# 96 unused bytes at the top of on-chip memory, which shift one half of the tiles against the other

## The chip, the cores and the metric

The kernel runs on one core of a Trainium2 chip. The metric is the device time of one launch in microseconds (us). Before the change the median of three runs is 1282.69 us (1281.51 to 1283.05). The engines are named as in the profile: PE is TensorE (matmul), PEld its loading of weights, DVE VectorE, ACT ScalarE, POOL GpSimd, SP SyncE, which issues most DMAs.

## The reference

One sequence of 256 tokens with 1024 features passes two transformer blocks, all in float32:

```
x = x + (sigmoid(ga) * (att @ w_att_o) + sigmoid(gr) * (ret @ w_ret_o)) @ w_out   # att, ret from rms_norm(x) @ w_in
x = x + (silu(h @ w_gate) * (h @ w_up)) @ w_down                                  # h = rms_norm(x), 2816 hidden
x = rms_norm(x)
x = x + concat(gated_mlp, banded_attention) @ w_out2                              # from rms_norm(x) @ w_in2
q = h @ w_query; top 16 of 128 x 128 sub-keys per head, 8 heads, softmax g         # h = rms_norm(x)
x = x + sum over the chosen experts of g * gelu(u_e . h) * v_e                     # 16384 experts
```

The last line is computed densely: every token meets all 16384 rows of `u` (the first layer), a gate that is zero for experts not chosen multiplies the result, and all 16384 rows of `v` follow (the second layer). Those two layers are 128 units of 128 experts each.

## The kernel before

**Three products for one.** A float32 matrix is split into two parts, `hi` (the value as the reduced float32 type that PE takes at full rate) and `lo` (the rest). A product of two such matrices is hi*hi + hi*lo + lo*hi. Weights come from memory in units of 128 x 1024 numbers: SP loads a unit into a `raw` tile (4 buffers), ACT copies it to `whi` (L95), DVE subtracts to get `wlo` (L96). Activations are split in the same way into pairs of tiles: `act`, `hid`, `att`, `xbh` and `xbl` in the stages up to the experts' first layer, `keys` and `q` in the second layer.

**Four shapes of matmul.** In each, one operand is loaded into PE beforehand (the stationary one, 128 x 128) and the other streams past it (the moving one, 128 x 256 or 128 x 512). The four shapes are called by letters from here on:

- **D**, `mm3` from `gemm_t` and `gemm_k` (L110 to L112): stationary `whi` or `wlo`, moving 256 columns of an activation. 24 of them per unit. It is the experts' first layer, the query product and a part of the other stages.
- **C**, `mm2` from `gemm_w` (L118, L119): stationary `whi`, moving 512 columns (hi and lo of an activation beside each other), then stationary `wlo`, moving 256 columns. Gates, gate/up/down of the feed-forward.
- **B**, `mm3` from `gemm_n` (L110 to L112 again, but with 512 columns): stationary an activation, moving 512 columns of `whi` or `wlo`.
- **A**, `second_layer` in `peer` (L1121): stationary `keys` or `q` (the gated activations), moving 512 columns of `whi` or `wlo`.

**Where tiles lie.** A partition of the on-chip memory is filled from both ends. Pools opened as usual lie at the low end, and pools opened under `using_default_side("right")` at the high end, each new one below the last. `run` opens the pool of weights `wb` first at the high end, and with it the `raw` tiles. Later high-end pools are `wa` (more weights), and in `peer` `gs`, `query` (with `keys` and `q`), `hold`, `topk`, `gelu`, `comb`, `gates` and the last `x3`. Activations (`act`, `hid`, `att`, `xbh`, `xbl`), residuals and the work tiles of blocks 1 and 2 are at the low end. All tiles that PE reads in the shapes A to D begin at a multiple of 256 bytes of their own half's start, so within a half their addresses agree modulo 256. In the program as it is built they are 0 modulo 256 for the low end and 224 modulo 256 for the high end (`whi` at byte 163808, for one). So the addresses of the shapes are, modulo 256:

| shape | moving | stationary | stationary minus moving |
|---|---|---|---|
| A | 224 | 224 | 0 |
| B | 224 | 0 | 32 |
| C, D | 0 | 224 | 224 (32 behind) |

**Order.** The order of work on each engine is set by a scheduler at build time from priorities; weights run ahead (`high_priority(offset=AHEAD)` in `unit`). The choice of experts on DVE is cut into steps, and `pump` lets a number of them out after each first-layer unit.

Of the kernel before, what the change touches and what calls it, by code (L numbers as in the profile page):

```python
# [7 lines left out]
F32 = mybir.dt.float32  # L8
# [35 lines left out]
class Net:  # L44
# [195 lines left out]
    def run(self):  # L240
        self.wpools, self.turn = [], 0
        with self.tc.using_default_side("right"):
            self.weights("wb", self.stack, 4, 3)
        self.xbp = self.pool("xb", 1)
        with ExitStack() as st:
            actp = self.pool("actp", 2, st)
            self.res = self.pool("res", 2, st)
            self.work = self.pool("work", 2, st)
            with ExitStack() as sw:
                with self.tc.using_default_side("right"):  # L250
                    self.weights("wa", sw, 0, 3)
                x2, h, acc, acg = self.block1(actp)
                x3, h, acc = self.block2(actp, x2, h, acc, acg)
            self.wpools.pop()
            self.peer(st, x3, h, acc)
# [985 lines left out]
```

## Time and profile before

| | |
|---|---|
| median of three runs | 1282.69 us |
| the profiled execution | 1281.63 us |
| its span | 1279.8 us |
| PE busy | 1269.9 us, 8408 matmuls |
| PEld busy | 1152.2 us, 8408 loads |
| DVE, ACT, POOL busy | 927.6, 740.0, 268.6 us |

The span runs from the first to the last record of the trace. A matmul's busy time is modelled and reaches past the start of the next, so the duration of one (279 to 391 ns) says little about its rate; the rate is read from the distance between the starts of matmuls that follow each other without a wait. In the views below a row of a window gives the number of matmuls that touch it. With a window of W and a duration d of one, that number times the distance between starts is W + d.

### The profile page before, as it was taken

The page shows a single profiled execution, that of the slowest core. Times are in us where ns is not written, and L with a number is a line of the kernel's source. Part 1 is how long each engine was busy: PE and PEld are TensorE (multiplying, and loading weights), DVE is VectorE, ACT ScalarE, POOL GpSimd, SP SyncE. Part 2 cuts the span into 40 slices and gives each one's busy share as a digit, 9 for nine tenths or more (in the row PEclk, how much of TensorE's full clock was granted, in tenths as well). Part 3 has the DMA queues.
Part 4 walks back from the last instruction along what each step waited for, and adds up shares of the span by engine and source line. Part 5 has one row for each costly group of instructions (what it writes and reads, how often), then busy time and mean ns, then how long its engine had stood idle before and what let it go on. Part 6 is the DMA issues. An engine that isn't in the chain of part 4 may idle for free.

```text
span 1279.8 us, 22295 instructions
## 1 busy us (share of the span) xinstructions
PE 1269.9 (99%) x8408; PEld 1152.2 (90%) x8408; DVE 927.6 (72%) x1857; ACT 740.0 (58%) x1238; POOL 268.6 (21%) x173
## 2 busy tenths in 40 slices
PE   8999999999999999999999999999999999999998
PEld 8978889888988889999999999999988888888887
DVE  7867787777777876987995566676566666666665
ACT  5555565655555776545554676666455555555553
POOL 2000000000000000018877778772000000000000
PEclk9999999999999999999999999999999999999999
DMA  7735558966667535567767677776666766666664
GB/s 242 268 132 165 181 182 324 315 193 189 180 186 225 162 111 164 173 193 191 184 158 209 182 169 179 165 169 179 217 216 214 219 220 219 215 219 219 221 198 157
DMA packets 91068, 252.94 MB, mean 198 GB/s; under 512 B 26960, under 2 KB 29008, under 8 KB 90832
## 3 DMA queue, kind: packets, MB, share of 16 engines
q1 hardware_dynamic: 68960, 241.58, 59.7%
q0 software_dynamic: 20992, 8.46, 6.0%
q8 instruction: 66, 1.08, 0.3%
q10 hardware_dynamic: 1008, 1.47, 0.3%
q14 instruction: 42, 0.34, 0.1%
HBM read 240.93 MB, written 10.55 MB: 196 GB/s over the span
## 4 chain that ended last, share of the span: by engine, by line
PE 94%; DVE 4%; DMA 1%; ACT 1%; issue 0%; DVEq 0%; ACTq 0%
PE ax L1121 27%; PE mm L110 15%; PE mm L112 14%; PE mm L111 14%; PE mm L118 13%; PE mm L119 7%; DVE wlo L96 1%; PE ax L994 1%; ACT whi L95 0%; PE ax L940 0%; DVE itop L793 0%; DMA x3t<-xt 0%; DMA small<-in_small_dram 0%; PE ax L484 0%; PE ax L730 0%
## 5 line engine op out<-in xcount | busy, mean ns | idle before, releaser
L96 DVE TENSOR_TENSOR wlo<-raw,whi 128x1024 fp32r<-128x1024 f32 (+2 forms) x433 | 524.2, 1213 | 235.3 <-ACT whi L95 233.5
L95 ACT ACTIVATE whi<-raw 128x1024 fp32r<-128x1024 f32 (+3 forms) x439 | 457.6, 1046 | 299.9 <-PE mm L111 133.9
L110 PE MATMUL mm<-xbh,whi 128*128 128x256 f32 x1104 | 311.9, 283 | 0.0
L112 PE MATMUL mm<-xbh,wlo 128*128 128x256 f32 x1104 | 308.3, 279 | 0.4 <-DVE wlo L96 0.3
L111 PE MATMUL mm<-xbl,whi 128*128 128x256 f32 x1104 | 308.3, 279 | 0.2 <-DVE xbl L177 0.2
L884 POOL DMA_INDIRECT cmat<-best,pos x128 | 240.6, 1880 | 221.2 <-DVE itop L793 161.6
L112 PEld LDWEIGHTS mm<-xbh,wlo 128*128 128x128 f32 x1104 | 207.4, 188 | 1.2 <-DVE wlo L96 1.0
L111 PEld LDWEIGHTS mm<-xbl,whi 128*128 128x128 f32 x1104 | 207.5, 188 | 0.4 <-DVE xbl L177 0.4
L110 PEld LDWEIGHTS mm<-xbh,whi 128*128 128x128 f32 x1104 | 207.6, 188 | 0.2 <-ACT xbh L176 0.2
L118 PE MATMUL mm<-act,whi 128*128 128x512 f32 x512 | 178.5, 391 | 0.0
L1121 PE MATMUL ax<-whi,q 128*128 128x512 f32 x513 | 158.2, 389 | 0.0
L1121 PE MATMUL ax<-wlo,keys 128*128 128x512 f32 x513 | 158.1, 389 | 0.0
L1121 PE MATMUL ax<-whi,keys 128*128 128x512 f32 x513 | 158.1, 389 | 0.0
L119 PE MATMUL mm<-act,wlo 128*128 128x256 f32 x512 | 144.4, 282 | 0.0
L176 ACT ACTIVATE keys<-S 128x256 fp32r<-128x256 f32 x128 | 53.4, 418 | 151.4 <-PE ax L1121 151.4
L118 PEld LDWEIGHTS mm<-act,whi 128*128 128x128 f32 x512 | 96.1, 188 | 20.4 <-DVE gu L132 0.3
L1121 PEld LDWEIGHTS ax<-whi,q 128*128 128x128 f32 x513 | 96.3, 188 | 20.0
L1121 PEld LDWEIGHTS ax<-wlo,keys 128*128 128x128 f32 x513 | 96.3, 188 | 19.9
L1121 PEld LDWEIGHTS ax<-whi,keys 128*128 128x128 f32 x513 | 96.2, 188 | 19.9
L119 PEld LDWEIGHTS mm<-act,wlo 128*128 128x128 f32 x512 | 96.8, 189 | 0.0
L111 PE MATMUL mm<-act,whi 128*128 128x256 f32 x328 | 91.9, 281 | 2.3 <-DVE act L275 2.3
L110 PE MATMUL mm<-act,whi 128*128 128x256 f32 x328 | 92.9, 284 | 0.8 <-DVE qkv L314 0.6
(291 smaller groups left out, 1667.5 us busy)
## 6 DMA issues: line engine op xcount, KB each, us to landing
raw<-in_peer_u_dram SPq DMA_DIRECT2D x128, 512.0 KB, 3.7
raw<-in_peer_v_dram SPq DMA_DIRECT2D x128, 512.0 KB, 4.2
raw<-in_w_in_b_dram SPq DMA_DIRECT2D x32, 512.0 KB, 4.5
raw<-in_w_in_a_dram SPq DMA_DIRECT2D x31, 512.0 KB, 3.6
raw<-in_w_gate_dram SPq DMA_DIRECT2D x22, 512.0 KB, 5.5
raw<-in_w_up_dram SPq DMA_DIRECT2D x22, 512.0 KB, 4.2
raw<-in_w_out_dram SPq DMA_DIRECT2D x16, 512.0 KB, 4.3
cmat<-zero SPq DMA_DIRECT2D x16, 512.0 KB, 6.8
```

Of the source, the lines that this page charges most:

```text
L95: self.last_copy = nc.scalar.activation(hi[:, s], raw[:, s], AF.Copy).ins
L96: low = (engine or nc.vector).tensor_tensor(out=lo[:, s], in0=raw[:, s], in1=hi[:, s].bitcast(F32), op=OP.subtract)
L110: mm(ps, lhsT=left[0], rhs=right[0], start=first, stop=False)
L111: mm(ps, lhsT=left[0], rhs=right[1], start=False, stop=False)
L112: mm(ps, lhsT=left[1], rhs=right[0], start=False, stop=last)
L118: mm(ps, lhsT=weight[0], rhs=both, start=first, stop=False)
L119: mm(ps[:, :T], lhsT=weight[1], rhs=both[:, 0], start=False, stop=last)
L176: nc.scalar.activation(hi, src, AF.Copy)
L884: i = nc.gpsimd.indirect_dma_start(self.cmat, bass.IndirectOffsetOnAxis(ap=ps[:, hd, 1, k:k + 1], axis=0), bs[:, hd, 1, k:k + 1], None, co ...
L994: nc.tensor.matmul(C[:, t * 128:t * 128 + 128], lhsT=A[:, t], rhs=G[i][:, t], start=i == 0, stop=i == 1)
L1121: nc.tensor.matmul(banks[tb][o // 512][:, o % 512:o % 512 + e - o], lhsT=s[left][:, ts], rhs=w[right][:, o:e], start=first, stop=end and e ...
```

## The change

Before the first high-end pool is opened, one more is opened there, with one tile of 24 float32 numbers (96 bytes) in each partition. Nothing writes or reads it. It stays open to the end.

```diff
         with self.tc.using_default_side("right"):
+            self.pool("edge", 1).tile([128, 24], F32, name="edge")
             self.weights("wb", self.stack, 4, 3)
```

All tiles of the high end move down by 96 bytes and nothing else moves: `whi` from byte 163808 to 163712, `keys` from 182240 to 182144, `raw` from 212960 to 212864. High-end tiles are now 128 modulo 256. The instructions on every engine, their order and their waits are those of the kernel before, one for one. The table becomes:

| shape | moving | stationary | stationary minus moving |
|---|---|---|---|
| A | 128 | 128 | 0 |
| B | 128 | 0 | 128 |
| C, D | 0 | 128 | 128 |

## Rows read from the trace of the kernel before

**Rows 1.** The page's head and busy time by engine, and the granted clock

```profile
span 1279.8 us, 22295 instructions
PE 1269.9 (99%) x8408; PEld 1152.2 (90%) x8408; DVE 927.6 (72%) x1857; ACT 740.0 (58%) x1238; POOL 268.6 (21%) x173
...
PEclk9999999999999999999999999999999999999999
```

**Rows 2.** Waits of PE: for whom, us in total, times, longest

```profile
PE mm L111 <- DVE act L275: 2.3, 3, 1.0
PE ax L221 <- ACT dg L220: 1.1, 1, 1.1
PE ax L59 <- DVE ones L54: 1.1, 1, 1.1
```

**Rows 3.** The chain that ended last, shares by engine (page)

```profile
PE 94%; DVE 4%; DMA 1%; ACT 1%; issue 0%; DVEq 0%; ACTq 0%
```

**Rows 4.** Windows, PE alone: window, length, busy (matmuls), clock, DMA share, GB/s

```profile
412.00:434.00 22.00, 22.00 (x96) 1.00 0.56 167
590.00:610.00 20.00, 20.00 (x174) 1.00 0.77 190
902.00:926.00 24.00, 24.00 (x208) 1.00 0.71 222
930.00:1270.00 340.00, 340.00 (x1501) 1.00 0.67 213
...
```

**Rows 5.** The same view of a window of shape C

```profile
232.00:332.00 100.00, 100.00 (x579) 1.00 0.70 221
```

**Rows 6.** Timeline of PE: 16 f16 matmuls of 128 columns and the next

```profile
744.67 1.07 PE L994 MATMUL ax<-G,A 128*128 128x128 f16 x16
745.55 0.36 PE L110 MATMUL mm<-xbh,whi 128*128 128x256 f32 x1
```

**Rows 7.** Groups of DVE by shape, the same operation into high-end and low-end tiles

```profile
L177 DVE TENSOR_TENSOR q<-S,keys 128x256 fp32r<-128x256 f32 x128 | 54.1, 423 | 38.0 <-ACT keys L176 38.0
...
L177 DVE TENSOR_TENSOR hid<-y,hid 128x256 fp32r<-128x256 f32 x22 | 9.1, 419 | 1.0 <-ACT hid L176 1.0
```

**Rows 8.** The chain that ended last, in order of time: start us, us, what

```profile
927.69 347.51 PE ax L1121 x1533
...
```

**Rows 9.** Groups of PE by shape: count, busy us, mean ns, idle before

```profile
L110 PE MATMUL mm<-xbh,whi 128*128 128x256 f32 x1104 | 311.9, 283 | 0.0
L112 PE MATMUL mm<-xbh,wlo 128*128 128x256 f32 x1104 | 308.3, 279 | 0.4 <-DVE wlo L96 0.3
L111 PE MATMUL mm<-xbl,whi 128*128 128x256 f32 x1104 | 308.3, 279 | 0.2 <-DVE xbl L177 0.2
L118 PE MATMUL mm<-act,whi 128*128 128x512 f32 x512 | 178.5, 391 | 0.0
...
L110 PE MATMUL mm<-act,whi 128*128 128x256 f32 x328 | 92.9, 284 | 0.8 <-DVE qkv L314 0.6 <-ACT act L274 0.2
...
L118 PE MATMUL mm<-hid,whi 128*128 128x512 f32 x176 | 61.1, 390 | 0.0
L110 PE MATMUL mm<-whi,act 128*128 128x512 f32 x128 | 51.4, 401 | 0.0
...
L118 PE MATMUL mm<-att,whi 128*128 128x512 f32 x32 | 11.4, 390 | 0.0
...
L110 PE MATMUL ax<-act,whi 128*128 128x256 f32 x24 | 6.9, 287 | 0.0
```

**Rows 10.** Windows of all engines in the choice of experts: PE, PEld, DVE, ACT, POOL

```profile
515.00:540.00 25.00, 24.79 (x209) 24.28 (x208) 24.66 (x114) 14.17 (x22) 0.00 (x0) 1.00 0.56 170
...
611.00:633.00 22.00, 22.00 (x190) 22.00 (x189) 21.32 (x86) 12.21 (x16) 18.95 (x11) 1.00 0.72 175
638.00:660.00 22.00, 22.00 (x189) 22.00 (x189) 22.00 (x95) 10.65 (x13) 16.57 (x8) 1.00 0.69 174
```

**Rows 11.** Timeline of PE: first and last of six A matmuls of 256 columns

```profile
1275.03 0.28 PE L1121 MATMUL ax<-whi,keys 128*128 128x256 f32 x1
...
1275.62 0.28 PE L1121 MATMUL ax<-whi,q 128*128 128x256 f32 x1
```

## The prediction

> **What bounds the kernel now.** I read the busy times and the granted clock first: PE is busy for 1269.9 of 1279.8 us, and its clock is at full speed throughout [rows 1], so no stage runs at the lower level. The waits of PE come next: its three longest entries sum to 4.5 us [rows 2]. The chain of waits gives PE 94% and DVE 4% [rows 3]. So the time is the sum of the distances between the starts of matmuls, and only something that changes these distances, or the little that DVE holds up, can move it.
>
> The distances are read from windows that hold one shape alone (window plus one duration, divided by the count). D: 20.28 us over 174 is 116.6 ns, and 24.28 over 208 is 116.7 [rows 4]. A: 340.39 over 1501 is 226.8 ns [rows 4]. B: 22.40 over 96 is 233.3 ns [rows 4]. C: 100.33 us over 579 is 173.3 ns on average, which is 346.6 for a pair of 512 and 256 columns [rows 5].
>
> What would they be without a loss? Columns at 2.4 GHz, the level that is granted, take 213.3 ns for 512, 106.7 for 256 and 53.3 for 128. The 16 f16 matmuls of 128 columns start within 745.55 - 744.67 = 0.88 us, 55.0 ns each, so 1.7 ns over their columns [rows 6]. As an estimate from that row I take 215.0, 108.4 and, for a pair, 323.4 ns as the distances without loss. What is lost for each matmul is then 8.3 ns in D, 23.2 per pair in C, 18.3 in B and 11.8 in A.
>
> The point on which the change turns is that A and B differ. Both stream 512 columns of `whi` or `wlo` past a stationary operand of 128 x 128 of the same type, at the same clock, with no wait; yet B takes 6.5 ns more. In A the two operands agree modulo 256 bytes, in B the stationary one is 32 bytes on. There are other differences (which output bank comes next, how often one stationary operand is used in a row), so this is not proof; but it is what one would see if PE's load of the next weights and its stream of moving columns got in each other's way by their addresses.
>
> **The change part by part.** It adds a tile that no instruction touches, so no instruction, no DMA and no wait is added, removed or moved on any queue, SP's and POOL's included. What it does is to move all high-end tiles by 96 bytes. The effects by reader:
>
> - DVE and ACT read and write high-end tiles at 128 instead of 224 modulo 256. The same subtraction takes 423 ns into `q` at the high end and 419 into `hid` at the low end [rows 7], so their place costs 4 ns at the most, on engines with idle time. I cost it at nothing; if all 128 of these took 4 ns more or less it would be 0.5 us on DVE, under PE's 347.5 us of A [rows 8]. The loads of `raw` move in the same way, behind four buffers; nothing shown bounds their change but the fact that PE waits for no load now [rows 2], and I cost it at nothing.
> - A: both operands move together and stay 0 apart. 1533 matmuls of 512 columns in 347.51 us [rows 8] keep their 226.7 to 226.8 ns. Zero.
> - D, C and B come to 128 apart, a distance that no stream of this trace has. The counts are 3 x (1104 + 328 + 24) = 4368 matmuls in D, 512 + 176 + 32 = 720 pairs in C, 3 x 128 = 384 in B [rows 9]. The upper bound of the gain is that the whole loss goes: 4368 x 8.3 = 36.3, 720 x 23.2 = 16.7, 384 x 18.3 = 7.0, together 60.0 us. On the other side, the nearest rows at other distances are B's 18.3 ns for one matmul at 32 apart: with that in D and C the loss grows by 4368 x 10.0 = 43.7 and 720 x 13.4 = 9.6, together 53 us. So the bounds are -60 and +53.
>
> Between them I take half of the loss gone, -30 us. The reason: all distances in this trace (0, 32 on, 32 behind) are close together, and all of them pay. 128 is the farthest that two streams can start from each other if the pattern repeats every 256 bytes. The moving stream still passes the load's position while it runs (512 columns are 2048 bytes, a load 512 bytes per partition), so I do not take the whole.
>
> Not all of that reaches the end. While experts are chosen, DVE is busy for 24.66 of 25 us, 21.32 of 22 and 22.00 of 22 in three windows [rows 10], so their 209 + 190 + 189 = 588 matmuls cannot come sooner: 588 x 4.15 = 2.4 us of D's half are lost, since DVE is what is late next there. The sum is -30.0 + 2.4 = -27.6 us against the profiled execution's own 1281.6 us: 1254.0. The median of the runs is 1.1 us above that execution, so 1255 us.
>
> A rule of the Trainium skill speaks against all this. The rows are 226.8 ns for A and 233.3 for B [rows 4]. The page "SBUF — State Buffer", section "Who interferes with whom", gives PE two read ports, one for the moving operand and one for the loading of weights, calls them independent, and says "PE and ACT never wait on anyone". By that rule the distance between the operands has no effect and the sum is zero instead of -27.6. The rows agree with it in so far as neither DVE, ACT nor DMA shows in the distances (D has 116.6 ns with DMA at 0.77 and 116.7 with it at 0.71); they do not where A and B part.
>
> **The rivals.**
>
> *No change.* The difference between A and B comes from something else than addresses, or the moving stream, which passes through every distance while a load runs, pays the same from wherever it starts. For it: C and A lose the same per matmul (23.2 / 2 = 11.6 and 11.8) though their distances are 224 and 0. Against it: B. The time stays at 1281.6 to 1282.7; with B alone falling to A's distance it is 384 x 6.5 = 2.5 us less, about 1280. The rule of the Trainium skill quoted above is of this kind.
>
> *Slower: 128 apart is where the load and the stream meet.* One mechanism: in the time of a load of 512 bytes per partition the moving operand goes through 1024 or more, so they pass each other, and from which start they meet most often is not known; B shows that 32 bytes can cost 6.5 ns. The place is D, C and the price by the nearest rows: the 512-column half of C at 6.5 ns more, 720 x 6.5 = 4.7 us, and D at the highest distance that 256 columns show anywhere, the last six of A with (1275.62 - 1275.03) / 5 = 118.0 ns [rows 11], 4368 x 1.3 = 5.7 us; together 1292, or 1293 on the scale of the medians. With 6.5 ns in D and both halves of C it would be 4368 x 6.5 + 720 x 13 = 37.8 us more, 1320. It decides as soon as D's distance is over 116.7 ns. Against it: A at distance 0 and C at 32 behind lose the same, so the cost does not jump with every step of 32 bytes.
>
> *The change does not do what it says.* A scheduler could have taken another order or the pad could be rounded away. The built program has the shifted addresses and the same order and waits, so I give this nothing.
>
> **How the numbers follow.** Forecast (part of the loss goes) 0.55; no change 0.16; slower 0.29. What a measurement of this kernel can tell from no change is about 0.2%, 2.6 us. Nearly all of the forecast's cases are faster by more than that, the slower rival's by more on the other side; so faster 0.55, same 0.16, slower 0.29. The forecast's own range is 1230 (all of the loss but what DVE holds back, 1281.6 - 60 + 5, and the 1.1 to the median, is 1228) to 1277. The slower rival goes on from 1286 to 1320; I let the range reach to 1296, which leaves out its upper half and the last of the full gain, about 0.15 to 0.2.
>
> **What would show it.** In the profile after, the windows of one shape alone: D should be at about 112.5 ns, a pair of C at 335, B at 224, A unchanged at 226.8; durations of DVE and ACT unchanged; PE's busy share still 99%, with DVE a little more of the chain of waits between 515 and 680 us. D at 116.7 would be the first rival, D over 117 the second. The forecast is wrong in its ground if A moves too: then it is the place itself and not the distance between operands that counts.

## The result: slower by 0.9%, and the profile after

The changed kernel takes 1293.86 us (median of four runs, 1291.93 to 1294.54) against 1282.56 for the kernel before on the same chip (1281.51 to 1283.05): a ratio of 1.0091 with a 95% interval of 1.0079 to 1.0103. The forecast was 1255 us. The time lies near the price of the slower rival, 1292 or 1293, and inside the stated range only because that was let reach into this rival's part.

The page after: head, busy time by engine, granted clock in 40 slices, and the chain's shares.

```profile
span 1292.7 us, 22295 instructions
PE 1284.7 (99%) x8408; PEld 1165.0 (90%) x8408; DVE 926.9 (72%) x1857; ACT 740.8 (57%) x1238; POOL 272.5 (21%) x173
...
PEclk8999999999999999999999999999999999999999
...
PE 98%; DMA 1%; DVE 1%; ACT 0%; issue 0%; DVEq 0%; ACTq 0%
```

The same instructions, the same busy DVE, ACT and POOL to within 4 us; PE alone has grown, by 14.8 us over 12.9 us of span [rows 1]. The 8 at the clock's start is a mean granted clock of 0.89 over the first 32 us (first window below); a later kernel of this study (`both_halves`) starts in the same way and has the span of the kernel before (1279.8 us), so it is not the cause. Nor does the chain's DVE share, 4% before [rows 3] and 1% now, say anything: that later kernel, with the time of the one before, has 97% PE and 2% DVE in its chain.

Waits of PE: for whom, us in total, times, longest.

```profile
PE mm L111 <- DVE act L276: 1.1, 2, 0.7
PE ax L59 <- DVE ones L54: 1.1, 1, 1.1
PE ax L221 <- ACT dg L220: 1.0, 1, 1.0
```

No wait is longer than in [rows 2], and the longest that is not shown is 0.6 us in both kernels. So the time went into the distances between starts. Windows that hold one shape each (window, length, PE busy with its matmuls, clock, DMA share, GB/s): the start, then D, C, D twice more, B and A.

```profile
0.00:32.00 32.00, 29.07 (x195) 0.89 0.72 239
...
200.00:220.00 20.00, 20.00 (x171) 1.00 0.93 336
235.00:335.00 100.00, 100.00 (x571) 1.00 0.69 220
590.00:610.00 20.00, 20.00 (x171) 1.00 0.80 203
...
690.00:710.00 20.00, 20.00 (x169) 1.00 0.70 183
417.00:438.00 21.00, 21.00 (x92) 1.00 0.57 171
945.00:1275.00 330.00, 330.00 (x1457) 1.00 0.69 219
```

By the prediction's rule (window plus one duration, over the count) D is 118.6 and later 120.0 ns, where it was 116.6 and 116.7 [rows 4]; a pair of C is 2 x 100.33 / 571 = 351.4, where it was 346.6 [rows 5]; B is 21.40 / 92 = 232.6 and A 226.8, where they were 233.3 and 226.8 [rows 4]. Over all matmuls of a shape the trace gives these means (of the distances that no wait has stretched) and totals:

| shape | distance mod 256 | before, ns | after, ns | total before, us | total after, us |
|---|---|---|---|---|---|
| D | 224 to 128 | 116.9 | 119.5 | 524.5 | 534.2 |
| C (pair) | 224 to 128 | 346.7 | 351.0 | 250.1 | 253.2 |
| B | 32 to 128 | 233.2 | 232.5 | 91.1 | 90.8 |
| A | 0 | 226.7 | 226.7 | 348.1 | 348.1 |

The totals hold the idle gaps of each shape as well, and that of A its six matmuls of 256 columns, which its mean leaves out. Their differences sum to 9.7 + 3.1 - 0.3 = +12.5 of the 12.9 us of span. The chain in order of time shows where (start us, us, what): attention products in the first B stretch at 79.20, token sums in a later B stretch, behind the last C, at 415.81, transposes right behind that stretch at 441.12, the start of A.

```profile
79.20 1.01 PE ax L531 x4
...
415.81 0.79 PE ax L210 x8
441.12 1.64 PE ax L629 x15
...
940.56 347.54 PE ax L1122 x1533
```

The same pieces of the kernel before started at 78.05, 411.04, 436.42 and 927.69 us (the last in [rows 8]): 1.2 us later at 79 (0.2 of it with the slower clock at the start: `both_halves` is at 78.24 there), 4.8 at 416, 4.7 at 441 (B gave a little back), 12.9 at A, and nothing more from there. The delay grows while D and C run, and stops when A begins.

DVE's group into `q` shows no effect of the place on that engine (line, shapes and count | busy us, mean ns | idle before):

```profile
L177 DVE TENSOR_TENSOR q<-S,keys 128x256 fp32r<-128x256 f32 x128 | 54.1, 424 | 38.2 <-ACT keys L176 38.2
```

424 ns against 423 [rows 7].

### The profile page after: what moved, and what is told of

It reads as the page before. It is cut to its first block, busy times and chain, and to the rows that moved or that the text cites. A ratio compares the mean times of both kernels' runs of the same rounds, so it can differ in the third digit from the quotient of the medians.

```text
span 1292.7 us, 22295 instructions
## 1 busy us (share of the span) xinstructions
PE 1284.7 (99%) x8408; PEld 1165.0 (90%) x8408; DVE 926.9 (72%) x1857; ACT 740.8 (57%) x1238; POOL 272.5 (21%) x173
## 4 chain that ended last, share of the span: by engine, by line
PE 98%; DMA 1%; DVE 1%; ACT 0%; issue 0%; DVEq 0%; ACTq 0%
PE ax L1122 27%; PE mm L110 16%; PE mm L111 15%; PE mm L112 15%; PE mm L118 13%; PE mm L119 7%; PE ax L995 1%; PE ax L941 0%; DMA small<-in_small_dram 0%; DMA x3t<-xt 0%; PE ax L485 0%; PE ax L731 0%; PE ax L110 0%; PE ax L766 0%; PE ax L531 0%; PE ax L111 0%
## 5 line engine op out<-in xcount | busy, mean ns | idle before, releaser
L112 PE MATMUL mm<-xbh,wlo 128*128 128x256 f32 x1104 | 313.5, 284 | 0.0
L111 PE MATMUL mm<-xbl,whi 128*128 128x256 f32 x1104 | 312.7, 283 | 0.2 <-DVE xbl L177 0.2
L885 POOL DMA_INDIRECT cmat<-best,pos x128 | 244.4, 1910 | 223.6 <-DVE itop L794 163.4
L110 PE MATMUL mm<-act,whi 128*128 128x256 f32 x328 | 94.7, 289 | 0.8 <-ACT whi L95 0.6
L111 PE MATMUL mm<-act,whi 128*128 128x256 f32 x328 | 93.8, 286 | 1.1 <-DVE act L276 1.1
```

The source lines that it names most:

```text
L110: mm(ps, lhsT=left[0], rhs=right[0], start=first, stop=False)
L111: mm(ps, lhsT=left[0], rhs=right[1], start=False, stop=False)
L112: mm(ps, lhsT=left[1], rhs=right[0], start=False, stop=last)
L885: i = nc.gpsimd.indirect_dma_start(self.cmat, bass.IndirectOffsetOnAxis(ap=ps[:, hd, 1, k:k + 1], axis=0), bs[:, hd, 1, k:k + 1], None, co ...
```

## The experiments

The theories at the outset: **distance** (what counts is how far, modulo 256 bytes, PE's load and its stream start apart, and 128 is a bad value), **place** (the high-end tiles themselves are worse where they are now), and for the form of the first, **valley** (loss falls smoothly with distance) or **spots** (single distances are good).

### The streams alone, 16 distances

A kernel without the network: one matmul stream after another, the moving operand shifted against the stationary one; the five parts are 256 columns, 512 columns, pairs, half a stationary operand (64 of 128 columns), and f16. `APART` is 0, 16 and so on to 240.

```diff
+    def stream(k, apart, n):
+        o = 2048 + (-apart % 256) // 4 + k % 4 * 1024
+        return big[:, o:o + n]
+    ...
+    for apart in APART:
+        ps = bank(f"d{apart:03d}x")
+        for k in range(48):
+            mm(ps[:, :256], lhsT=load(k), rhs=stream(k, apart, 256), start=True, stop=True)
```

> This kernel leaves the whole network out: it only streams matmuls, with no DVE, ACT or DMA work beside them, in segments that differ in one thing, the distance (stationary minus moving, modulo 256 bytes) from 0 to 240 in steps of 16: 48 of 256 columns (D), 32 of 512 columns (A and B), 24 pairs of 512 and 256 (C). At four distances also 48 of 256 columns with a stationary operand of half the columns, and 48 of 256 columns in f16. Theory 1, the load of the next weights and the moving stream disturb each other by their distance: D shows about 116.7 ns at 224 and 119.5 at 128, 512 columns about 227 at 0 and 233 at 32, a pair 346.7 at 224 and 351 at 128, each without any other engine at work; f16 shows no difference between distances, half a load loses about half. Theory 2, it is traffic of the other engines at shifted addresses: every segment of a shape has the same distance between starts, near 109 and 216 ns. Of the other distances I know nothing; I expect some under 116 ns for D.

PE's timeline (start us, us, line, output named by shape and distance, shapes, count). The distance between starts is the next row's start less this one's, over the count.

```profile
44.04 5.63 PE L74 MATMUL d064x<-big 128*128 128x256 f32 x48
49.51 5.88 PE L74 MATMUL d080x<-big 128*128 128x256 f32 x48
...
66.47 5.92 PE L74 MATMUL d128x<-big 128*128 128x256 f32 x48
72.22 5.66 PE L74 MATMUL d144x<-big 128*128 128x256 f32 x48
77.72 5.92 PE L74 MATMUL d160x<-big 128*128 128x256 f32 x48
...
100.57 5.82 PE L74 MATMUL d224x<-big 128*128 128x256 f32 x48
106.22 5.77 PE L74 MATMUL d240x<-big 128*128 128x256 f32 x48
111.83 7.44 PE L78 MATMUL a000x<-big 128*128 128x512 f32 x32
119.11 7.63 PE L78 MATMUL a016x<-big 128*128 128x512 f32 x32
126.58 7.63 PE L78 MATMUL a032x<-big 128*128 128x512 f32 x32
134.05 7.67 PE L78 MATMUL a048x<-big 128*128 128x512 f32 x32
```

(49.51 - 44.04) / 48 = 114.0 ns at 64; 119.8 at 128; 114.6 at 144; 117.7 at 224; for 512 columns 227.5 at 0 and 233.4 at 32. Without the first eight of each stream, which differ from the rest (at 144 it takes eleven, and then 113.3 stands):

| distance | 0 | 16 | 32 | 48 | 64 | 96 | 128 | 144 | 160 | 192 | 224 | 240 |
|---|---|---|---|---|---|---|---|---|---|---|---|---|
| 256 columns, ns | 120.0 | 117.1 | 118.3 | 119.1 | 113.3 | 117.3 | 120.0 | 113.8 | 120.0 | 117.8 | 117.8 | 116.6 |
| 512 columns, ns | 226.7 | 233.3 | 233.3 | 234.7 | 233.3 | 234.2 | 232.3 | 231.1 | 233.3 | 228.9 | 233.3 | 231.7 |
| pair, ns | 346.6 | 353.3 | 353.4 | 350.0 | 353.3 | 346.7 | 350.8 | 353.3 | 350.0 | 353.3 | 346.7 | 346.6 |

The kernel's distances come back with no other engine at work: A and B part at 0 and 32 as they do in the kernel, C has 346.7 at 224 and 350.8 at 128, D 117.8 and 120.0. So the addresses make the difference; no change of output bank or of the use of the operands is needed for it. No distance is good for all three shapes: 64 is the best for 256 columns and among the worst for a pair. Half a stationary operand, from its rows of the same view (the first two shown):

```profile
365.22 5.64 PE L87 MATMUL n000x<-big 128*64 128x256 f32 x48
370.70 5.77 PE L87 MATMUL n032x<-big 128*64 128x256 f32 x48
```

At 0 it settles at 113.3 ns after some 13 matmuls, where the whole operand takes 120.0; it takes 116.7 at 32 (118.3), 116.6 at 128 (120.0) and 117.9 at 224 (117.8). So it lost less at three of the four distances, by no fixed share; the expectation had half. And f16 does not care:

```profile
387.56 5.41 PE L92 MATMUL h000x<-half 128*128 128x256 f16 x48
392.81 5.40 PE L92 MATMUL h032x<-half 128*128 128x256 f16 x48
398.05 5.40 PE L92 MATMUL h128x<-half 128*128 128x256 f16 x48
403.29 5.40 PE L92 MATMUL h224x<-half 128*128 128x256 f16 x48
```

5.25 / 48 = 109.4 ns at 0 and 5.24 / 48 = 109.2 at 32 and 128.

### Both ends moved, the distance restored

The high end keeps its 96 bytes and all tiles of the low end are moved by 160, so that D, C and B are again 224 and 32 apart, with every address new.

```diff
             self.pool("edge", 1).tile([128, 24], F32, name="edge")
             self.weights("wb", self.stack, 4, 3)
+        self.pool("low", 1).tile([128, 40], F32, name="low")
```

> The changed kernel with 160 unused bytes at the low end too, below the activations, so that all distances are again those of before (A 0, B 32, C and D 224), while both halves begin at other addresses than before (128 and 160 modulo 256). Theory 1, the distance counts: back to 1282.6 us (1281 to 1284), D at 116.7 ns. Theory 2, the place of the high end itself counts (128 is worse than 224): it stays at 1294 (1292 to 1296).

1281.83 us against 1281.69, ratio 1.0001 (0.9992 to 1.0011), with D at 116.9, a pair at 346.7, B at 233.3. The chain in order of time:

```profile
927.61 347.51 PE ax L1123 x1533
```

A starts 0.08 us from where it did before the change [rows 8]. The place theory falls.

### 256 bytes more

```diff
-            self.pool("edge", 1).tile([128, 24], F32, name="edge")
+            self.pool("edge", 1).tile([128, 88], F32, name="edge")
```

> The changed kernel with 352 unused bytes in place of 96, which is 256 more: distances modulo 256 are those of the changed kernel, modulo 512 they are not. Theory 1 with a period of 256: 1294 us (1292 to 1296). A period of 512 or more, or none: another time, D not at 119.5 ns.

1291.62 us against 1281.69, ratio 1.0078 (1.0061 to 1.0095): the changed kernel's loss again (its interval, 1.0079 to 1.0103, overlaps with this one). A pair (351.0) and B (232.4) are the same, D is 118.8 instead of 119.5 in the profiled executions. That fits a period of 256; that one distance can have two values of D was not expected and is taken up below.

### Every distance at 0

The pad is 224 bytes, so that D, C and B come to the distance that A has.

```diff
-            self.pool("edge", 1).tile([128, 24], F32, name="edge")
+            self.pool("edge", 1).tile([128, 56], F32, name="edge")
```

> The changed kernel with 224 unused bytes in place of 96: all distances are 0. Theory 1: B falls from 233 to A's 226.8 ns (-2.5 us), D goes to what six matmuls of 256 columns showed at distance 0, 118.0 to 118.6 ns (+5.7 to +8.3 us against before), so 1286 to 1289 us. Theory 2 (place of the high end) says nothing but that it differs.

1291.5 us against 1281.69, ratio 1.0076 (1.006 to 1.0093), slower than the 1286 to 1289 expected. B fell to 227.7, near A's 226.7, but D went to 119.9 and a pair to 348.6. PE's windows, two of D as above with two of C between:

```profile
200.00:220.00 20.00, 20.00 (x169) 1.00 0.93 329
240.00:325.00 85.00, 85.00 (x492) 1.00 0.68 215
345.00:395.00 50.00, 50.00 (x285) 1.00 0.63 188
690.00:710.00 20.00, 20.00 (x169) 1.00 0.70 185
```

20.28 / 169 = 120.0 ns, the value of the bare stream at 0. The distance that is best for 512 columns is bad for 256. A pair is at 2 x 85.34 / 492 = 346.9 ns, near the bare stream's 346.6, and later at 2 x 50.34 / 285 = 353.3, which the bare stream at 0 did not show: a pair, too, can have two values at one distance.

### The streams alone, finer, with other sizes

The same kernel with distances 4 bytes apart around 64 and 128, streams that are entered again later, 256 to 1024 bytes more, and 128 to 448 columns.

```diff
+    def run(name, n, count, apart, step=1024, load_step=128):
+        ...
+    for i, apart in enumerate((0, 64, 128, 64, 224, 64)):
+        run(f"r{i}s{apart:03d}x", 256, 64, apart)
```

> Again streams of matmuls alone, the network left out. (1) 256 columns at distances 48 to 80 and 128 to 160 in steps of 4 bytes: if the loss follows the distance smoothly there is a valley around 64; if it hangs on a lock of load and stream that holds only in certain positions, 113.3 ns stands at some distances and 117 to 120 right beside them. (2) Distance 64 after distances 0, 128 and 224: 113.3 each time if the distance alone counts, different if the history does. (3) 64 and 128 with 256, 512, 768 and 1024 bytes more: the same as 64 and 128 if the pattern repeats every 256 bytes. (4) Steps between successive operands of 0 and of 2048 bytes: the same, if only the distance modulo 256 counts. (5) 128, 192, 320, 384 and 448 columns: if the loss belongs to each load, the distance between starts is columns / 2.4 GHz plus 4 to 20 ns whatever the number of columns; if it belongs to each column streamed, it grows with the number.

Not a valley: 256 columns take 120.6 ns at 56, 122.4 at 60, 113.3 at 64, 120.1 at 68; and 121.4 at 136, 122.6 at 140, 113.3 at 144, 120 at 148. The same distance entered at another time, in PE's timeline:

```profile
132.51 7.43 PE L77 MATMUL r1s064x<-big 128*128 128x256 f32 x64
139.78 7.76 PE L77 MATMUL r2s128x<-big 128*128 128x256 f32 x64
147.38 7.70 PE L77 MATMUL r3s064x<-big 128*128 128x256 f32 x64
154.92 7.63 PE L77 MATMUL r4s224x<-big 128*128 128x256 f32 x64
```

At 64 the first stream takes 7.27 / 64 = 113.6 ns, the second, after one at 128, 7.54 / 64 = 117.8. With 256 bytes and more in addition nothing changed: 64 took 117.7 to 117.9 five times, 128 took 120.0 four times, each group run in one go. Nor did steps of 0 or 2048 bytes between operands: 113.3 at 64 and 118.5 to 118.8 at 128, values that both have elsewhere. By columns, from rows of the same view, the least and the most of the distances 0, 64, 128 and 224, once steady: 128 and 192 columns 111.3 to 111.9, 320 columns 146.7 at all four, 384 columns 173.3 to 176.6, 448 columns 202.3 to 206.7. Fewer columns than 256 did not come below 111.3 ns, and from 320 to 448 each matmul is 13 to 20 ns over its columns at 2.4 GHz. The least of that does not grow with the columns (13.4, 13.3 and 15.6 ns): the loss goes with the matmul, which has one load, more than with the columns.

### 64 apart in D and C

```diff
-            self.pool("edge", 1).tile([128, 24], F32, name="edge")
+            self.pool("edge", 1).tile([128, 40], F32, name="edge")
```

> The changed kernel with 160 unused bytes: D and C at distance 64, B at 192, A at 0. If the distances between starts of the streams alone carry over into the kernel (D 113.3, pair of C 353.3, B 228.8, A 226.7), against before D is -3.6 x 4368 = -15.7 us, C +6.6 x 720 = +4.8, B -4.4 x 384 = -1.7: 1269 to 1272 us with what DVE holds back. Rival: the streams alone lock because nothing interrupts them; in the kernel D is broken up by waits and by other matmuls and stays at 117 to 120 ns: 1284 to 1300 us.

1278.42 us against 1282.32, ratio 0.9964 (0.9951 to 0.9978): faster, by less than half of what was expected. By the trace, D on `xb` (3312 of the 4368) is 7.4 us shorter with a mean of 114.0 ns, the other D at 115.7 saves 0.7, B at 229.2 saves 1.4, and C at 353.3 gives 4.6 back, as the map has it. That is -4.9 of the span's -4.3. The other D took 113.3 in some stretches (480 to 500 us) and 117.8 in others (190 to 220); and on `xb` the idle gaps grew from 5.3 to 7.7 us.

### 64 apart for `xb` alone

```diff
-            self.pool("edge", 1).tile([128, 24], F32, name="edge")
+            self.pool("edge", 1).tile([128, 40], F32, name="edge")
...
+            self.pool("low", 1, st).tile([128, 24], F32, name="low")
             actp = self.pool("actp", 2, st)
```

> 160 unused bytes at the high end and 96 at the low end between the experts' activations and all others: D of the experts' first layer and the queries' second part (3312 matmuls) at distance 64, all other D and C at 224 as before, B at 32 as before, A at 0. If distances carry over: -3.6 x 3312 = -11.9 us against before, 1270 to 1273 us. Rival (they do not): 1282 to 1295 us.

1274.48 us (1273.59 to 1276.12) against 1282.32, ratio 0.9939 (0.9925 to 0.9952): faster than both kernels, but short of the 1270 to 1273 expected. C and B stay at 347.0 and 233.3 (32 of the 720 pairs, on `att`, which takes `xbh`'s place early on, come to 64 as well). Windows of D on `xb`:

```profile
565.00:585.00 20.00, 20.00 (x179) 1.00 0.64 166
...
690.00:710.00 20.00, 20.00 (x172) 1.00 0.72 186
```

20.28 / 179 = 113.3 and 20.28 / 172 = 117.9 ns: one kernel, one code, one distance, and the two values that the bare stream at 64 has. The higher one stands at 541 to 549, 589 to 609 and 670 to 715 us, so the mean is 114.5; the idle gaps grew from 5.3 to 7.7 us.

### The change undone for `xb` alone

```diff
             self.pool("edge", 1).tile([128, 24], F32, name="edge")
             self.weights("wb", self.stack, 4, 3)
+        self.pool("low", 1).tile([128, 40], F32, name="low")
         self.xbp = self.pool("xb", 1)
...
+            self.pool("low2", 1, st).tile([128, 24], F32, name="low2")
             actp = self.pool("actp", 2, st)
```

> The change undone for one group of streams: 96 unused bytes at the high end, and low-end bytes such that the experts' activations (3312 matmuls D) are back at distance 224, while all other D, C and B keep 128. If each stream pays by its own distance, the 3312 fall from 119.5 to 116.9 ns and the time to 1293.9 - 8.6 = 1285 us (1284 to 1287), C stays at 351 a pair. If the place of the high end counted it would stay at 1294.

1286.44 us against 1282.32, ratio 1.0033 (1.002 to 1.0047). Windows of D before and in the experts:

```profile
200.00:220.00 20.00, 20.00 (x171) 1.00 0.98 338
565.00:585.00 20.00, 20.00 (x174) 1.00 0.72 212
```

118.6 ns where the distance is 128, 116.6 where it is back at 224. So `xb` makes up 7.2 of the 11.3 us between the medians (1293.86 - 1282.56, less 1286.44 - 1282.32), and the other D and C the rest; a pair is at 351.0 still.

### The streams alone, all 64 distances

Every distance in steps of 4, and four of them entered from seven others each.

```diff
+    for apart in range(0, 256, 4):
+        run(f"f{apart:03d}x", 256, 36, apart)
+    for goal in (64, 144, 224, 128):
+        for came in (0, 16, 32, 96, 128, 176, 224):
+            run(f"b{goal:03d}u{came:03d}x", 256, 16, came)
+            run(f"g{goal:03d}u{came:03d}x", 256, 32, goal)
```

> Streams of 256 columns alone, the network left out: first all 64 distances in steps of 4 bytes, then the distances 64, 144, 224 and 128, each entered from seven other distances. In the runs so far each distance had one or two steady values (64: 113.3 and 117.8; 128: 118.6 and 120.0; 224: 116.7 and 117.8; 144: 113.3 both times). If a steady value is a lock between load and stream that the history picks, 64 shows both of its values here, 224 and 128 theirs, and no third one. If 144 has but one lock, 113.3 stands after each of the seven. Rival, that the value depends on the distance alone and the second value came from something else: one value per distance.

Of the 64, 113.3 ns shows at 144 alone (64 was at 117.8 this time), 116.6 to 116.8 at 196 and 224, and the other 60 lie between 117.1 and 123.5. The distance before the change was among the best four in this pass. But 112 and 240, at 116.7 and 116.6 in the first of these kernels, were at 118.5 and 118.7 here: they have two values as well. PE's timeline of entries (u and three digits: the distance before):

```profile
304.77 3.93 PE L77 MATMUL g064u016x<-big 128*128 128x256 f32 x32
308.54 2.06 PE L77 MATMUL b064u032x<-big 128*128 128x256 f32 x16
310.43 3.82 PE L77 MATMUL g064u032x<-big 128*128 128x256 f32 x32
314.09 2.04 PE L77 MATMUL b064u096x<-big 128*128 128x256 f32 x16
...
439.25 3.96 PE L77 MATMUL g128u128x<-big 128*128 128x256 f32 x32
443.05 2.07 PE L77 MATMUL b128u176x<-big 128*128 128x256 f32 x16
444.95 4.00 PE L77 MATMUL g128u176x<-big 128*128 128x256 f32 x32
448.80 2.04 PE L77 MATMUL b128u224x<-big 128*128 128x256 f32 x16
```

64 entered from 16 takes 3.77 / 32 = 117.8, from 32 it takes 3.66 / 32 = 114.4 (113.3 once the first few are past); 128 entered from itself 118.8, from 176 120.3. Of seven entries each, 64 took 113.3 six times and 117.8 once, 224 took 116.7 six times and 117.8 once, 128 took 118.4 to 118.8 six times and 120.0 once, and 144 took 113.3 all seven times. So the history matters, but the distance just before does not settle it: 64 entered from 128 took 117.8 in the finer map above (`r3s064x`) and 113.3 here, and from 224 likewise.

### 144 apart for `xb` alone

No pad at the high end; `xb` is moved at the low end, by 64 bytes of a pad and 16 inside its tiles.

```diff
-            self.pool("edge", 1).tile([128, 24], F32, name="edge")
+        self.pool("low", 1).tile([128, 16], F32, name="low")
         self.xbp = self.pool("xb", 1)
+            self.pool("low2", 1, st).tile([128, 48], F32, name="low2")
...
-        xb = [self.xbp.tile([128, 8, T], F32R, tag=t, name=t, bufs=1) for t in ("xbh", "xbl")]
+        xb = [self.xbp.tile([128, 8 * T + 64], F32R, tag=t, name=t, bufs=1)[:, 4:8 * T + 4].rearrange(
+            "p (k t) -> p k t", k=8) for t in ("xbh", "xbl")]
```

> No unused tile at the high end; low-end bytes put the experts' activations (3312 matmuls D) at distance 144 and leave all else at the distances of before. If 144 locks at 113.3 ns in the kernel too, and more often than 64 did (114.5 ns on average, 1274.5 us): -3.6 x 3312 = -11.9 us and some held back by DVE, 1271 to 1274 us. If the lock at 144 needs an undisturbed stream (it took up to 11 matmuls at 117 to 126 ns to come): 1275 to 1285 us.

1274.81 us (1274.48 to 1275.71) against 1282.11, ratio 0.9945 (0.9931 to 0.9958): no better than `split`, and between the two ranges expected. D on `xb` settled at 113.3 everywhere and never at a second value (mean 113.9 with the first matmuls after each break), so its matmuls without the gaps are 3312 x 3.1 = 10.3 us shorter. But its idle gaps grew from 5.3 to 8.0 us, in the choice of experts. Windows: a steady one of D, PE alone, then one of that choice with PE, PEld, DVE, ACT, POOL:

```profile
690.00:710.00 20.00, 20.00 (x179) 1.00 0.76 200
```

```profile
638.00:660.00 22.00, 21.81 (x190) 21.46 (x190) 22.00 (x95) 10.45 (x13) 16.86 (x8) 1.00 0.71 176
```

DVE is busy for 22.00 of 22 us and PE no longer, at 21.81; before, PE was busy for all 22 there [rows 10]. This is the cover that the prediction named. The gaps took 2.7 us more; of that, the waits of PE that the profile names account for 1.6 (DVE's `wlo` from 0.3 to 1.4 us, ACT's `whi` from none to 0.5), so that DVE took all of it is not shown.

## Why the prediction was wrong, point by point

- **What bounds the kernel: right.** The sum of distances is the time: the ledger by shape gives 12.5 of 12.9 us with no wait of PE over 1.1 us.
- **The cause that A and B were read for: right.** The bare streams show 226.7 at 0 and 233.3 at 32 with everything else alike, and both ends moved at an unchanged distance give 1.0001. So the first rival (no change, A and B part for another reason) falls. The Trainium skill's page "SBUF — State Buffer", section "Who interferes with whom", agrees in so far as the other engines make no difference to PE (350.8 ns for a pair at 128 alone, 351.0 beside them all); it has no room for an effect of the distance between PE's own two operands, and 113.3 to 123.5 ns for one and the same matmul of 256 columns decides against that part.
- **"Half of the loss goes, because 128 is the farthest": this is the step that failed.** It took the loss for something that falls with the distance, and forecast 112.5 ns for D and 335 for a pair where 119.5 and 351.0 were measured. The loss has no such form: in the map of all 64, 61 distances lie at 117.1 to 123.5 ns, with 113.3 only at single points and 122.4 four bytes beside one. A trend was made from three distances, none of them seen in more than two shapes.
- **The distance without loss, 108.4 ns, and with it the bound of -60 us: wrong for this type.** It was worked out from f16 matmuls [rows 6]. f16 does show 109.2 ns, at all four distances tried; the kernel's own type reached 113.3 at best. What was really to be had by distances: 4368 x (116.9 - 113.3) = 15.7 us in D, 384 x (233.2 - 226.7) = 2.5 in B, and nothing in C, which stood at the best of its 16 distances: 18 us, not 60.
- **The slower rival: its mechanism in so far as the distance decides, its place (D and C), and its point of decision (D over 116.7 ns) held.** Its price was 5.7 + 4.7 = 10.4 us; measured are 9.7 + 3.1 = 12.8, less 0.3 in B. D is now at 119.5, over the 118.0 of [rows 11], which by the unrounded starts is 118.6, one distance of 114 ns and four of 119 to 120; in C both halves grew by some 2.2 ns, not one by 6.5. That the total came close is in part luck: D cost more than priced and C less. That load and stream *meet* at 128, the picture behind it, is not shown: no run looked at what inside PE waits.
- **Zero for A, for DVE and ACT, for the loads: right** (347.54 us for A, 424 ns for `q`, no load among PE's waits).
- **DVE late in the choice of experts: right where there was a gain to lose** (up to 2.7 us in the last experiment, 2.4 forecast for another gain), without object in the changed kernel, where PE is the slower one.

What stays open is why a distance has the value it has, and what picks one of two. The changed kernel's D lies for the most part at 118.4 to 118.8 ns until about 640 us and at 120.0 to 120.3 after; with 256 bytes more it is mostly at 118.6 after 670 us too. No run shows what chooses.

## What to carry to other kernels

Where PE is the bound and no wait is left, read the distance between starts by shape, and find out with a kernel of bare streams, of the same type and sizes, what each distance of operands modulo 256 bytes costs; it can't be guessed from two or three distances, while one such kernel of 416 us showed 128 and 144 for what they are. Enter each distance more than once, since some have two values. Then move only the stream that gains: `xb` alone at 64 or 144 gave 0.6%, all operands together 0.4% at 64 and a loss of 0.8 to 0.9% at 128 or 0. And bound "what could be gained at most" from rows of the same type.

## What the hardware showed that was not expected

- Matmuls of this four-byte type, granted full speed and with no wait: 256 columns take from 113.3 to 123.5 ns, 512 columns from 226.7 to 234.7, a pair from 346.6 to 353.4, in streams that differ only in the distance between the stationary and the moving operand. f16: 109.2 at 0, 32, 128 and 224.
- Some distances have two steady values: for 256 columns 64 has 113.3 and 117.8, 128 has 118.6 and 120.0, 224 has 116.7 and 117.8; for a pair 0 has 346.6 and 353.3. What ran before can change which one is taken, and a kernel can go from one to the other in its course.
- With a stationary operand of 64 columns 256 moving columns took 113.3 ns at 0 and 116.6 at 128, where 128 stationary columns took 120.0 at both in the same kernel, but 117.9 at 224 (117.8). 128 or 192 moving columns did not come below 111.3 ns a matmul.
